# A two-layer encoder trunk: the second FFN product in one chunk of eleven tile pairs, with right factors kept in DRAM

## The chip, the cores and the metric

The kernel runs on one core of a Trainium2 chip. The metric is device microseconds (us) of one execution. TensorE (PE) multiplies, PEld is its weight load, VectorE is DVE, ScalarE is ACT, GpSimd is POOL and SyncE is SP; SyncE's queue issues nearly all DMAs.

## The reference, cut to what matters

The trunk has two layers on a sequence of 1024 tokens of width 1024, in float32. A layer is a normalisation, a projection into three kinds of mixers, an output projection, and then the part in which the change lies (`D_FF` is 2816, that is 22 tiles of 128):

```
h = rmsnorm(x, ffn_norm[i])
gu = h @ w_up[i]
x = x + (jax.nn.silu(gu[..., :D_FF]) * gu[..., D_FF:]) @ w_down[i]
x = x + (p[i] @ ple_proj[i]) * jax.nn.sigmoid(x @ ple_gate[i])
```

## The kernel before, in words

Everything is held transposed: features on the 128 partitions, tokens on the free axis in two halves of 512. A float32 operand is split into two parts of the type fp32r (`split`, L131): ScalarE casts the high part (L133), VectorE or, where `eng` says so, GpSimd subtracts it from the source to give the low part (L134). A product of two split operands takes three matmuls of 128 x 128 by 128 x 512, high by high, high by low and low by high (L1409 to L1411, and L219 to L221 in `product`).

The first FFN product (`feed` L1417, `up` L1285) makes one tile f of the 22 at a time. It uses a seven-product scheme on 2 x 2 blocks: seven sums (`part`, L1262) of 12 matmuls in place of eight. `factors` makes the seven left factors of the next tile meanwhile: its sums on GpSimd (L191 to L200), its splits on ScalarE and VectorE, in slots `wf` of the pool `big` (16 slots of 128 x 1024). For the tiles one to three the first two sums are made early (`heads`), so that five remain. The gated product of a tile, two halves of 128 x 512, is stored to the DRAM tensor `gd` (L1306).

The second FFN product (`lower`, L1309) is also made by seven products, on pairs of tiles, in two chunks of ten tiles (`NDOWN`). A chunk has the products 1, 2, 7, 5, 6, 3 and 4, each over five pairs, and a step (chunk, product, pair) is 12 matmuls into four PSUM banks. `fetch` loads the blocks of w_down (`a11` to `a22`, the left side) and of the gated product (`b11` to `b22`, the right side). `factors` inside `lower` forms a step's sums of blocks (L1336), `ready` splits the left one with GpSimd and the right one with VectorE, and the loop runs `ready` three steps (`DEEP`) ahead of the matmuls. After a product, `out` adds the four banks to blocks of x or to `sums` (L1382), and after product six of the second chunk adds `sums` to three blocks each (L1393). The two tiles left over are multiplied plainly, 96 matmuls (L219 to L221 with `g` and `wh`, added at L1479); at the end of this each block of x is split into `xp`, the right side of the gate's product that follows (`pe` and `pd` with `xp`).

Each engine runs its own queue in a fixed order. Tiles of a pool share its slots; a new tile waits until the last reader of the slot's former one is done. The framework orders the queues when the kernel is built, from the order of the code, its own estimates of durations and the free slots, so loads and splits can stand far ahead of where the code has them: loads of x that `lower` issues (L1376) go out while the first product still runs. SyncE's DMA instructions wait on SyncE's queue for their sources or slots, and those behind them wait too.

Of the kernel before, what the change touches and what calls it, by code (L numbers as in the profile page):

```python
# [21 lines left out]
P = 128  # L22
# [17 lines left out]
NDOWN = 10  # L40
# [42 lines left out]
class Trunk:  # L83
# [236 lines left out]
    def scratch(self):  # L320
        self.xd = self.dram.tile([KT, P, S], F32, name="xd")
        self.ya = self.dram.tile([3, P, S], F32, name="ya")
        self.yd = self.dram.tile([S, HC * HD], F32, name="yd")
        self.sgd = self.dram.tile([3, P, S], F32, name="sgd")
        self.gd = self.dram.tile([NFF, P, S], F32, name="gd")
        self.md = self.dram.tile([64, S], F32, name="md")
        self.ad = self.dram.tile([64, NCH], F32, name="ad")
# [704 lines left out]
    def plan_all(self):  # L1032
        t = self.t
        for li in range(DEPTH):
# [8 lines left out]
            for i in range(2):  # L1043
                self.plan((4, 256), t["w_last"][li, 4 * i : 4 * i + 4].rearrange("f p c -> p f c"))
# [240 lines left out]
    def up(self, rt, f, ops, gu):  # L1285
# [18 lines left out]
        for hf, (g, t) in enumerate(((g0, u), (g1, v))):  # L1304
            add(g, g, t, OP.mult)
            nc.sync.dma_start(self.gd[f][:, hf * 512 : hf * 512 + 512], g)  # L1306
        yield

    def lower(self, li, x, gp):  # L1309
# [4 lines left out]
        K2 = NDOWN // 2  # L1314
        where = {"11": (0, h0), "12": (K2, h0), "21": (0, h1), "22": (K2, h1)}
        raw = {}

        def fetch(c, *names):
            for k in range(K2):
                for n in names:  # L1320
                    if n in ("a12", "a22"):
                        if k % 2 == 0:
                            pair = self.slot("wr")
                        w = pair[:, k % 2 * 512 : k % 2 * 512 + 512]
                    else:
                        w = self.rhs.tile([P, 512], F32, tag="hl", name=self.nm("wr"))
                    if n[0] == "a":
                        k0, cs = where[n[1:]]
                        nc.sync.dma_start(w, t["w_down"][li, c * NDOWN + k0 + k, :, cs])
                    else:  # L1330
                        k0, cs = {"11": (0, h0), "12": (0, h1), "21": (K2, h0), "22": (K2, h1)}[n[1:]]
                        nc.sync.dma_start(w, self.gd[c * NDOWN + k0 + k][:, cs])
                    raw[c, n, k] = w

        def sub(out, a, b, eng=nc.vector, op=OP.subtract):
            eng.tensor_tensor(out, a, b, op)  # L1336
            return out

        def factors(c, m, k):

            g = lambda n: raw[c, n, k]
            p = lambda n: raw.pop((c, n, k))
            if m == 1:
                return g("a11"), g("b11")
            if m == 2:
                return g("a12"), g("b21")
            if m == 7:
                return sub(self.half("s"), g("a11"), g("a21")), sub(self.half("s"), g("b22"), g("b12"))
            if m == 5:
                return (sub(g("a21"), g("a21"), g("a22"), op=OP.add), sub(g("b12"), g("b12"), p("b11")))  # L1350
            if m == 6:
                return sub(g("a11"), p("a21"), g("a11")), sub(g("b12"), g("b22"), g("b12"))
# [4 lines left out]
        def ready(c, m, k):  # L1357
            l, r = factors(c, m, k)
            out = []
            for src, eng in ((l, nc.gpsimd), (r, nc.vector)):  # L1360
                pair = tuple(gp.tile([P, 512], F32R, tag="hl", name=self.nm("f")) for _ in range(2))
                self.split(pair, src, eng=eng)
                out.append(pair)
            if m == 3:
                raw.pop((c, "a12", k)), raw.pop((c, "b22", k))
            if m == 4:
                raw.pop((c, "a22", k)), raw.pop((c, "b21", k)), raw.pop((c, "b12", k))
            if k == K2 - 1 and c == 0:
                fetch(1, *{5: ("b11",), 6: ("a11",), 3: ("b21", "a12"), 4: ("a21", "b22", "b12", "a22")}.get(m, ()))
            return out  # L1370

        fetch(0, "a11", "b11")
        fetch(0, "a12", "b21")
        x += [self.slot("x") for _ in range(KT)]
        for o in range(KT):
            nc.sync.dma_start(x[o], self.xd[o])  # L1376
        us = [self.slot("u") for _ in range(2)]
        fetch(0, "a21", "b22", "b12", "a22")
        sums = [us[o // 2][:, o % 2 * 512 : o % 2 * 512 + 512] for o in range(4)]
# [4 lines left out]
        def out(c, m, o, ps):  # L1384
            c11, c12, c21, c22 = x[o][:, h0], x[o][:, h1], x[o + 4][:, h0], x[o + 4][:, h1]
            if m == 1 and c == 0:
# [9 lines left out]
        ahead = []  # L1396
        for i in range(len(steps) + DEEP):
            if i < len(steps):
                ahead.append(ready(*steps[i]))
            if i < DEEP:  # L1400
                continue
            c, m, k = steps[i - DEEP]
            if k == 0:
                odd = ((i - DEEP) // K2) % 2
                banks = [self.bank("pd", "d" if odd and o > 1 else "a") for o in range(4)]
            (lh, ll), (rh, rl) = ahead.pop(0)
            for o, ps in enumerate(banks):
# [3 lines left out]
                nc.tensor.matmul(ps, ll[:, cs], rh, start=False, stop=k == K2 - 1)  # L1411
            del lh, ll, rh, rl
            if k == K2 - 1:
                for o, ps in enumerate(banks):
                    out(c, m, o, ps)

    def feed(self, li, x, acc, rt, gp, fill):  # L1417
# [19 lines left out]
        x.clear()  # L1437
        for f in range(NFF):
# [13 lines left out]
        self.lower(li, x, gp)  # L1452
        self.limit = 1 << 30
        gs = self.pairs(2, "g", gp)
        for f, g in enumerate(gs):
            for hf in hs:
                gr = self.half("gr")
                nc.sync.dma_start(gr, self.gd[2 * NDOWN + f][:, hf * 512 : hf * 512 + 512])
                self.split(g[hf], gr)

        pp = self.pairs(PLE // P, "p", gp)
        for k in range(PLE // P):
            for hf in hs:
                pr = self.half("pr")
                nc.sync.dma_start(pr, t["p"][li, k, :, hf * 512 : hf * 512 + 512])
                self.split(pp[k][hf], pr)
        pw = self.pairs(2, "pw", gp)
        for i in range(4):
            pr = self.half("pr")
            nc.sync.dma_start(pr.rearrange("p (f c) -> p f c", f=2), t["ple_proj"][li, 2 * i : 2 * i + 2].rearrange("f p c -> p f c"))  # L1470
            self.split(pw[i // 2][i % 2], pr)
        xp = [[None, None] for _ in range(KT)]
        hl = [self.take(), self.take()]
# [193 lines left out]
```

## Time and profile before

| | |
|---|---|
| median of 3 runs (lowest to highest) | 2799.74 us (2798.83 to 2800.63) |
| the profiled execution, its span | 2797.81 us, 2796.0 us |
| PE busy, share of the span | 2670.7 us, 96% |
| DVE, ACT, POOL busy | 1920.4, 1129.1, 966.8 us |
| mean granted TensorE clock | 0.978 |
| DMA traffic | 258.57 MB, mean 92 GB/s |

Busy is the union of an engine's instructions. Matmuls overlap in their pipeline, so their starts tell the pace better than their durations. In the profile L1306 is line 1306 of the kernel. A wait is idle time of an engine in front of an instruction, put down to the instruction that ended it.

### The profile page before, as it was taken

What the parts mean: (1) busy time and instruction counts of PE and PEld (TensorE: products, weight loads), DVE (VectorE), ACT (ScalarE), POOL (GpSimd) and SP (SyncE); (2) the same over time, 40 slices, a digit from 0 to 9 for tenths busy, and PEclk for the clock granted to TensorE, in tenths of its full rate; (3) what the DMA queues carried; (4) which work ended last, traced back from release to release, by engine and by line L of the source; (5) the groups of instructions that cost most, each with busy time, mean ns of one, the idle gap of its engine ahead of it and who ended that gap; (6) DMA issues with size and microseconds to landing.
All of it is one profiled execution on the core that took longest, in us unless ns stands there. A gap on an engine that the chain in (4) does not pass through costs nothing.

```text
span 2796.0 us, 37474 instructions
## 1 busy us (share of the span) xinstructions
PE 2670.7 (96%) x13930; PEld 2124.0 (76%) x13930; DVE 1920.4 (69%) x3019; ACT 1129.1 (40%) x2301; POOL 966.8 (35%) x724
## 2 busy tenths in 40 slices
PE   8999998998999999999999999989899999989997
PEld 6777776676888887788777778857678888877887
DVE  8654866579665558997655448564986565599957
ACT  5443253544333324344445433543443333333444
POOL 3112433136332325660121123431553333276302
PEclk9999999999999999999999999999899999999999
DMA  4010145132222235312321012542232222632124
GB/s 146 28 65 31 42 110 174 56 129 72 95 77 82 91 109 189 116 61 68 114 82 54 32 38 71 116 148 97 79 113 76 83 91 72 207 133 86 46 83 136
DMA packets 134618, 258.57 MB, mean 92 GB/s; under 512 B 14649, under 2 KB 55649, under 8 KB 134436
## 3 DMA queue, kind: packets, MB, share of 16 engines
q1 hardware_dynamic: 130740, 244.51, 26.7%
q0 software_dynamic: 3696, 11.66, 1.2%
q8 instruction: 110, 1.80, 0.3%
q14 instruction: 72, 0.59, 0.1%
HBM read 206.19 MB, written 49.93 MB: 92 GB/s over the span
## 4 chain that ended last, share of the span: by engine, by line
PE 77%; DVE 12%; issue 4%; POOL 2%; ACT 2%; DMA 2%; SPq 0%; DVEq 0%; POOLq 0%; ACTq 0%
PE pd L219 10%; PE pd L220 9%; PE pd L221 9%; PE pd L1270 9%; PE pd L1269 9%; PE pd L1271 9%; PE pd L1410 3%; PE pd L1411 3%; PE pd L1409 3%; PE po L584 1%; PE ppt L563 1%; DVE f L134 1%; DVE x L1234 1%; DVE x L1382 1%; DVE wr L1336 1%
## 5 line engine op out<-in xcount | busy, mean ns | idle before, releaser
L1270 PE MATMUL pd<-r,wf 128*128 128x512 f32 x1232 | 494.0, 401 | 16.4 <-POOL r L1229 9.3
L1269 PE MATMUL pd<-r,wf 128*128 128x512 f32 x1232 | 490.1, 398 | 11.3 <-ACT r L1228 11.3
L1271 PE MATMUL pd<-r,wf 128*128 128x512 f32 x1232 | 488.9, 397 | 0.0
L219 PE MATMUL pd<-h,wh 128*128 128x512 f32 x832 | 339.3, 408 | 12.7 <-ACT h L133 6.8
L220 PE MATMUL pd<-h,wh 128*128 128x512 f32 x832 | 329.4, 396 | 2.8 <-DVE h L134 1.7
L221 PE MATMUL pd<-h,wl 128*128 128x512 f32 x832 | 328.0, 394 | 1.0 <-DVE wl L134 1.0
L1288 DVE TENSOR_TENSOR g<-g,pd 128x512 f32<-128x512 f32 x264 | 176.8, 684 | 219.0 <-PE pd L1271 218.9
L1270 PEld LDWEIGHTS pd<-r,wf 128*128 128x128 f32 x1232 | 234.7, 191 | 81.7 <-POOL r L1229 19.2
L1269 PEld LDWEIGHTS pd<-r,wf 128*128 128x128 f32 x1232 | 235.1, 191 | 67.0 <-ACT r L1228 13.0
L1271 PEld LDWEIGHTS pd<-r,wf 128*128 128x128 f32 x1232 | 235.3, 191 | 52.3
L134 POOL TENSOR_TENSOR f<-wr,f 128x512 fp32r<-128x512 f32 x120 | 181.2, 1523 | 154.7 <-ACT f L133 127.9
L1410 PE MATMUL pd<-f,f 128*128 128x512 f32 x560 | 221.3, 395 | 12.9 <-DVE f L134 12.9
L1409 PE MATMUL pd<-f,f 128*128 128x512 f32 x560 | 220.3, 393 | 5.4 <-DVE x L1382 5.4
L1411 PE MATMUL pd<-f,f 128*128 128x512 f32 x560 | 220.8, 394 | 4.2 <-POOL f L134 4.1
L133 ACT CAST f<-wr 128x512 fp32r<-128x512 f32 x240 | 137.9, 619 | 192.6 <-PE pd L1410 90.7
L133 ACT CAST wf<-s 128x512 fp32r<-128x512 f32 x176 | 105.0, 619 | 272.4 <-POOL s L200 121.1
L134 DVE TENSOR_TENSOR wf<-s,wf 128x512 fp32r<-128x512 f32 x176 | 176.2, 1002 | 42.8 <-ACT wf L133 41.6
L134 POOL TENSOR_TENSOR wl<-wr,wh 128x1024 fp32r<-128x1024 f32 (+1 forms) x44 | 109.3, 2483 | 249.9 <-ACT wh L133 139.5
L219 PEld LDWEIGHTS pd<-h,wh 128*128 128x128 f32 x832 | 158.0, 190 | 48.1 <-ACT h L133 6.8
L220 PEld LDWEIGHTS pd<-h,wh 128*128 128x128 f32 x832 | 158.0, 190 | 35.2 <-DVE h L134 2.6
L221 PEld LDWEIGHTS pd<-h,wl 128*128 128x128 f32 x832 | 157.7, 189 | 35.5 <-DVE wl L134 1.9
L197 POOL TENSOR_TENSOR s<-wr,s 128x512 f32<-128x512 f32 x44 | 59.1, 1344 | 307.1 <-DVE wf L134 307.1
(315 smaller groups left out, 5484.2 us busy)
## 6 DMA issues: line engine op xcount, KB each, us to landing
wr<-w_up SPq DMA_DIRECT2D x88, 512.0 KB, 3.7
wr<-w_in SPq DMA_DIRECT2D x52, 512.0 KB, 3.6
gd<-g SPq DMA_DIRECT2D x88, 256.0 KB, 2.0
wr<-w_down SPq DMA_DIRECT2D x80, 256.0 KB, 4.2
wr<-gd SPq DMA_DIRECT2D x80, 256.0 KB, 5.3
wr<-ple_gate SPq DMA_DIRECT2D x40, 512.0 KB, 3.5
ee<-md SPq DMA_DIRECT2D x32, 384.0 KB, 7.5
x<-xd SPq DMA_DIRECT2D x24, 512.0 KB, 4.3
```

The source lines that it names most:

```text
L133: self.pin(nc.scalar.copy(hi[:, cs], src))
L134: self.pin((eng or nc.vector).tensor_tensor(lo[:, cs], src, hi.bitcast(F32)[:, cs], OP.subtract))
L219: nc.tensor.matmul(ps, hi[:, ks], rh, start=k == 0, stop=False)
L220: nc.tensor.matmul(ps, hi[:, ks], rl, start=False, stop=False)
L221: nc.tensor.matmul(ps, lo[:, ks], rh, start=False, stop=k == n - 1)
L1269: nc.tensor.matmul(ps, hi[:, ks], rh, start=k == 0, stop=False)
L1270: nc.tensor.matmul(ps, hi[:, ks], rl, start=False, stop=False)
L1271: nc.tensor.matmul(ps, lo[:, ks], rh, start=False, stop=k == KT // 2 - 1)
L1288: add = lambda out, a, b, op=OP.add: nc.vector.tensor_tensor(out, a, b, op)
L1409: nc.tensor.matmul(ps, lh[:, cs], rh, start=k == 0, stop=False)
L1410: nc.tensor.matmul(ps, lh[:, cs], rl, start=False, stop=False)
L1411: nc.tensor.matmul(ps, ll[:, cs], rh, start=False, stop=k == K2 - 1)
```

## The change

The second product becomes one chunk of eleven pairs: tiles 2k and 2k + 1 form pair k, and the plain product of two tiles with its weights (`w_last`) is gone. The four sums of right blocks are no longer formed in `lower`. As soon as both tiles of a pair are gated, the generator `rights`, which runs in steps beside the next tile's sums, stores the raw blocks `b11`, `b21` and `b22` to the DRAM tensor `bd`, forms the four sums on VectorE, splits them on ScalarE and VectorE and stores them to the DRAM tensor `bs`. In `lower`, `right` loads a raw block into a half slot (products 1, 2 and 3, split there) or a made and split factor straight into `f` tiles (products 7, 5, 6 and 4), one step ahead of `ready`. The left splits and the left subtractions of product 3, on GpSimd before, are on VectorE. x is loaded in eight parts during the first two products. The embedding's operands, the first loads of the gate's weights and twelve of sixteen `xp` splits are made beside product four (`beside`), the last four `xp` splits after it.

```
+    def rights(self, i):
+        (b11, b12), (b21, b22) = self.gated
+        for n, b in enumerate((b11, b21, b22)):
+            nc.sync.dma_start(self.bd[i, n], b)
+        yield
+        for n, (out, a, b) in enumerate(((None, b22, b12), (b12, b12, b11), (b12, b22, b12), (b21, b21, b12))):
+            w = self.slot("wf", F32R)
+            hl = w[:, 0:512], w[:, 512:1024]
+            out = hl[1].bitcast(F32) if out is None else out
+            nc.vector.tensor_tensor(out, a, b, OP.subtract)
+            self.split(hl, out)
+            nc.sync.dma_start(self.bs[i, n], w.bitcast(F32))
+            yield
...
+        def left(m, k):
...
+            if m == 7:
+                return sub(self.half("s"), g("a11"), g("a21"))
+            if m == 5:
+                return sub(g("a21"), g("a21"), g("a22"), OP.add)
+            if m == 6:
+                return sub(g("a11"), p("a21"), g("a11"))
             if m == 3:
-                return sub(g("a12"), g("a12"), p("a11"), nc.gpsimd), g("b22")
-            return g("a22"), sub(g("b21"), g("b21"), g("b12"), nc.gpsimd)
+                w = p("a12")
+                return sub(w, w, p("a11"))
+            return p("a22")
+        def right(m, k):
+            if m in (1, 2, 3):
+                r = self.half("b")
+                nc.sync.dma_start(r, self.bd[k, m - 1])
+                return r
+            hl = tuple(gp.tile([P, 512], F32R, tag="hl", name=self.nm("f")) for _ in range(2))
+            for w, cs in zip(hl, (h0, h1)):
+                nc.sync.dma_start(w.bitcast(F32), self.bs[k, {7: 0, 5: 1, 6: 2, 4: 3}[m]][:, cs])
+            return hl
...
-            for src, eng in ((l, nc.gpsimd), (r, nc.vector)):
-                pair = tuple(gp.tile([P, 512], F32R, tag="hl", name=self.nm("f")) for _ in range(2))
-                self.split(pair, src, eng=eng)
+            for src in (left(m, k), r):
+                if not isinstance(src, tuple):
+                    pair = tuple(gp.tile([P, 512], F32R, tag="hl", name=self.nm("f")) for _ in range(2))
+                    self.split(pair, src)
...
-            for dst in {1: (sums[o], c11)[c == 0 :], 2: (c11,), 7: (c21, c22), 5: (c12, c22), 6: (sums[o],), 3: (c12,),
-                        4: (c21,)}[m]:
+            for dst in {1: (c11,), 2: (c11,), 7: (c21, c22), 5: (c12, c22), 3: (c12,), 4: (c21,)}.get(m, ()):
                 add(dst, ps)
-            if m == 6 and c == 1:
+            if m == 6:
+                add(sums[o], ps)
                 for dst in (c21, c12, c22):
-                    nc.vector.tensor_tensor(dst, dst, sums[o], OP.add)
-        steps = [(c, m, k) for c in range(2) for m in (1, 2, 7, 5, 6, 3, 4) for k in range(K2)]
+                    add(dst, sums[o])
+        steps = [(m, k) for m in (1, 2, 7, 5, 6, 3, 4) for k in range(NPAIR)]
...
+            if i + 1 < len(steps):
+                rs.append(right(*steps[i + 1]))
             if i < len(steps):
-                ahead.append(ready(*steps[i]))
+                ahead.append(ready(*steps[i], rs.pop(0)))
+                m, k = steps[i]
+                if m in (1, 2, 7):
+                    fetch({1: "a12", 2: "a21", 7: "a22"}[m], k)
+                if m in (1, 2) and k < 4:
+                    stream(4 * (m - 1) + k)
+            elif i == len(steps):
+                next(beside)
...
+                if m == 3:
+                    next(beside)
...
             for _ in self.up(rt, f, ops[-5:], gu):
                 next(fill, None)
+                next(rights, None)
             drain(fill)
+            drain(rights)
+            if f % 2:
+                rights = self.rights(f // 2)
+        drain(rights)
...
-                drain(self.product(hl[o // 4], gs, hf, ps, (o % 4) * 256))
-                nc.vector.tensor_tensor(x[o][:, cs], x[o][:, cs], ps, OP.add)
...
+        self.lower(li, x, gp, beside())
+        for o in range(4, KT):
+            operand(o, 0)
```

## Rows read from the trace of the kernel before

**Rows 1.** The page's busy times: engine, busy us, share of the span, instructions.
```profile
PE 2670.7 (96%) x13930; PEld 2124.0 (76%) x13930; DVE 1920.4 (69%) x3019; ACT 1129.1 (40%) x2301; POOL 966.8 (35%) x724
```

**Rows 2.** VectorE's timeline, first product: start, us, instruction, [idle before].
```profile
873.39 1.79 DVE L134 TENSOR_TENSOR wf<-s,wf 128x512 fp32r<-128x512 f32 x1
...
876.12 0.69 DVE L1282 TENSOR_TENSOR g<-g,pd 128x512 f32<-128x512 f32 x1 [0.34 <-PE pd L1271]
...
895.45 0.69 DVE L1282 TENSOR_TENSOR g<-g,pd 128x512 f32<-128x512 f32 x1 [0.34 <-PE pd L1271]
```

**Rows 3.** TensorE's timeline: first matmuls of second and gate's products.
```profile
1063.79 0.39 PE L1409 MATMUL pd<-f,f 128*128 128x512 f32 x1
...
1293.92 0.39 PE L219 MATMUL pe<-p,pw 128*128 128x512 f32 x1
...
2432.34 0.39 PE L1409 MATMUL pd<-f,f 128*128 128x512 f32 x1
...
2661.26 0.39 PE L219 MATMUL pe<-p,pw 128*128 128x512 f32 x1
```

**Rows 4.** Groups, whole span: xcount, busy us, mean ns, idle us before.
```profile
L1409 PE MATMUL pd<-f,f 128*128 128x512 f32 x560 | 220.3, 393 | 5.4 <-DVE x L1382 5.4
...
L219 PE MATMUL pd<-g,wh 128*128 128x512 f32 x64 | 25.3, 395 | 0.0
```

**Rows 5.** TensorE's waits, second product, layers 0 and 1: us, times, longest.
```profile
PE pd L1410 <- DVE f L134: 6.2, 4, 3.8
PE pd L1409 <- DVE x L1382: 3.3, 1, 3.3
PE pd L1411 <- POOL f L134: 2.7, 3, 1.3
...
PE pd L1410 <- DVE f L134: 6.7, 5, 2.6
PE pd L1409 <- DVE x L1382: 2.1, 1, 2.1
PE pd L1411 <- POOL f L134: 1.4, 2, 1.0
```

**Rows 6.** Second product: length, busy (count) of PE, PEld, DVE, ACT, POOL, clock, DMA.
```profile
1060.00:1272.00 212.00, 199.75 (x860) 162.10 (x860) 202.37 (x231) 87.98 (x154) 134.58 (x88) 0.98 0.33 110
```

**Rows 7.** Groups in the second product of layer 0, 1064 to 1271 us.
```profile
L134 POOL TENSOR_TENSOR f<-wr,f 128x512 fp32r<-128x512 f32 x56 | 85.0, 1531 | 41.2 <-ACT f L133 28.4 <-DVE f L134 7.2 <-DVE wr L1336 1.7
L134 DVE TENSOR_TENSOR f<-wr,f 128x512 fp32r<-128x512 f32 x56 | 63.4, 1148 | 1.4 <-ACT f L133 1.4
...
L1336 DVE TENSOR_TENSOR wr<-wr,wr 128x512 f32<-128x512 f32 x40 | 44.2, 1128 | 0.4
```

**Rows 8.** VectorE's timeline, second product, layer 0.
```profile
1244.09 2.98 DVE L1393 TENSOR_TENSOR x<-x,u 128x512 f32<-128x512 f32 x3
...
1265.92 2.48 DVE L134 TENSOR_TENSOR g<-gr,g 128x512 fp32r<-128x512 f32 x4
```

**Rows 9.** Stretches, columns as in rows 6: two of the first product, two later.
```profile
673.00:718.00 45.00, 45.00 (x195) 36.61 (x196) 39.92 (x53) 16.96 (x31) 22.65 (x17) 1.00 0.33 113
850.00:869.33 19.33, 19.33 (x86) 15.77 (x85) 11.53 (x17) 6.01 (x10) 6.27 (x4) 1.00 0.22 81
...
1233.50:1272.00 38.50, 38.50 (x172) 31.86 (x171) 35.93 (x48) 18.85 (x32) 13.47 (x10) 1.00 0.27 83
...
1030.00:1090.00 60.00, 60.00 (x264) 49.21 (x263) 39.08 (x44) 20.52 (x36) 22.39 (x15) 1.00 0.79 270
```

**Rows 10.** SyncE's queue in the first product.
```profile
875.85 0.81 SPq L157 DMA_DIRECT2D wr<-w_up  x2
```

**Rows 11.** DMA issues, 672 to 1064 us: count, KB each, median us to landing.
```profile
wr<-w_up SPq DMA_DIRECT2D x36, 512.0 KB, 3.7
...
wr<-gd SPq DMA_DIRECT2D x11, 256.0 KB, 6.5
```

**Rows 12.** GpSimd's timeline in the first product.
```profile
892.28 1.68 POOL L191 TENSOR_TENSOR s<-wr 128x512 f32<-128x512 f32 x1 [1.46 <-DVE wf L134]
```

More of the change, by code (lines that the diff above doesn't have):

```diff
@@ L324, in scratch @@
         self.sgd = self.dram.tile([3, P, S], F32, name="sgd")
-        self.gd = self.dram.tile([NFF, P, S], F32, name="gd")
+        self.bd = self.dram.tile([NPAIR, 3, P, 512], F32, name="bd")
+        self.bs = self.dram.tile([NPAIR, 4, P, S], F32, name="bs")
         self.md = self.dram.tile([64, S], F32, name="md")
@@ L1312, in lower @@
+    def lower(self, li, x, gp, beside):
         nc, t = self.nc, self.t
         h0, h1 = slice(0, 512), slice(512, 1024)
-        K2 = NDOWN // 2
-        where = {"11": (0, h0), "12": (K2, h0), "21": (0, h1), "22": (K2, h1)}
         raw = {}
[L1318 to L1333, printed above, removed]
@@ L1335, in sub, with place, fetch @@
-        def sub(out, a, b, eng=nc.vector, op=OP.subtract):
-            eng.tensor_tensor(out, a, b, op)
-            return out
-        def factors(c, m, k):
-            g = lambda n: raw[c, n, k]
-            p = lambda n: raw.pop((c, n, k))
+        spare = []
+        def place():
+            if not spare:
+                pair = self.slot("wr")
+                spare.extend((pair[:, h1], pair[:, h0]))
+            return spare.pop()
+        def fetch(n, k):
+            w = place() if n == "a22" or (n, k) == ("a12", NPAIR - 1) else self.rhs.tile([P, 512], F32, tag="hl", name=self.nm("wr"))
+            nc.sync.dma_start(w, t["w_down"][li, 2 * k + int(n[2]) - 1, :, h0 if n[1] == "1" else h1])
+            raw[n, k] = w
@@ new lines, in ready @@
+        def ready(m, k, r):
+            out = []
+            for src in (left(m, k), r):
+                if not isinstance(src, tuple):
+                    pair = tuple(gp.tile([P, 512], F32R, tag="hl", name=self.nm("f")) for _ in range(2))
+                    self.split(pair, src)
+                    src = pair
+                out.append(src)
+            return out
+        for k in range(NPAIR):
+            fetch("a11", k)
+        us = [self.slot("u") for _ in range(2)]
+        sums = [us[o // 2][:, o % 2 * 512 : o % 2 * 512 + 512] for o in range(4)]
@@ L1482, in feed, with operand, beside @@
-        del gs, hl
+        xp = [[None, None] for _ in range(KT)]
+        def operand(o, hf):
+            xp[o][hf] = tuple(self.rhs.tile([P, 512], F32R, tag="hl", name=self.nm("xp")) for _ in range(2))
+            self.split(xp[o][hf], x[o][:, hf * 512 : hf * 512 + 512])
+        pp, pw = [], []
+        def beside():
+            prs = []
+            for k in range(PLE // P):
+                for hf in hs:
+                    prs.append(self.half("pr"))
+                    nc.sync.dma_start(prs[-1], t["p"][li, k, :, hf * 512 : hf * 512 + 512])
+            for o in range(4):
+                for hf in hs:
+                    operand(o, hf)
+            for o in range(4, KT):
+                operand(o, 1)
+            yield
+            self.limit = 1 << 30
+            self.load(self.njob)
+            pp.extend(self.pairs(PLE // P, "p", gp))
+            for k in range(PLE // P):
+                for hf in hs:
+                    self.split(pp[k][hf], prs.pop(0))
+            pw.extend(self.pairs(2, "pw", gp))
+            for i in range(4):
+                pr = self.half("pr")
+                nc.sync.dma_start(pr.rearrange("p (f c) -> p f c", f=2), t["ple_proj"][li, 2 * i : 2 * i + 2].rearrange("f p c -> p f c"))
+                self.split(pw[i // 2][i % 2], pr)
+            yield
@@ L1485, in feed @@
+        self.lower(li, x, gp, beside())
+        for o in range(4, KT):
+            operand(o, 0)
         hn = [[None, None] for _ in range(KT)]
```

86 lines of the change are left out of this document (24 added, 62 removed).

## The prediction

> **What bounds the kernel now.** I read the busy times first, then where the two FFN products begin and end, then TensorE's waits in them, then what the engine that it waits for is doing. TensorE is busy for 96% of the span [rows 1]. A sum of matmul durations would overstate its work, because matmuls overlap; what counts is start to start. In the first FFN product one tile's 84 matmuls recur every 895.45 - 876.12 = 19.33 us [rows 2], so one matmul costs 19.33 / 84 = 0.2301 us. In the second product that pace isn't held. With the plain product behind it, it runs in layer 0 from 1063.79 to 1293.92, 230.13 us, and in layer 1 from 2432.34 to 2661.26, 228.92 us [rows 3]. Each layer has 936 matmuls there: three lines of 560 and three of 64 for both layers [rows 4]. At 0.2301 us that is 215.4 us, so 14.7 us and 13.5 us, together 28.2 us, are lost. The waits name their cause: 12.2 us in layer 0 and 10.2 us in layer 1 end on a VectorE or GpSimd split or on a VectorE addition [rows 5]; the rest is matmuls at a reduced pace behind them (granted clock 0.98 over the stretch [rows 6]). The engine that is short is VectorE, busy for 202.4 of 212 us, beside a GpSimd busy for 134.6 us [rows 6].
>
> **The change, part by part.** *Fewer matmuls.* Eleven pairs in one chunk make 7 x 11 x 12 = 924 matmuls for 936. Two layers save 24 x 0.2301 = 5.5 us, all on the path.
>
> *VectorE and GpSimd in the second product.* GpSimd's 70 splits of some 1.53 us and its 20 subtractions go. VectorE's split averages 1.15 us there and its subtraction 1.13 us [rows 7]; where GpSimd rests, four splits take 2.48 us, 0.62 us each [rows 8]. The new stage issues on VectorE 77 left and 33 right splits, 44 left subtractions, 48 additions (twelve per output block where 22 were), 16 splits for the gate's product, 8 for the embedding, and 8 operations of the last pair's right factors: 234 x 0.62 = 145 us of 924 x 0.2301 = 212.6 us, 68% where it was 95%. A step of twelve matmuls (2.76 us) has at most three of them, 1.9 us, in product three; product seven's step had two subtractions and a split, 3.4 us, and additions besides. So the cause of [rows 5] goes. ScalarE has some 142 operations of about 0.62 us, 88 us, as now [rows 6].
>
> One rule of the Trainium skill bears on that price. The row first: the same split takes 0.62 us alone [rows 8] and 1.15 us on average beside GpSimd [rows 7]. "SBUF — State Buffer", section "Who interferes with whom", says that a VectorE instruction with two SBUF inputs and a GpSimd instruction that reads SBUF contend for a port pair held as an exclusive lock, and that the second to issue waits for the whole of the first. By that rule the 0.62 us holds in the second product, where GpSimd falls silent, but not in the first, where GpSimd still works; what would follow there is rival B.
>
> *Right factors in the first product.* Every pair of tiles adds four subtractions and four splits on VectorE. Alone they cost 8 x 0.62 = 5.0 us; each caught beside GpSimd, as a split of 1.79 us [rows 2], 14.3 us. VectorE is busy 11.53 of 19.33 us per tile [rows 9], so a pair has 15.6 us free: even the dear end fits. GpSimd works 6.27 of the 19.33 us, a third, so I take 5.0 us plus a third of the difference, 8 us, and at this place no time. What covers it: six PSUM banks take the sums, and weight splits stand ahead of their use. The exception is the start: from 673 to 718 us VectorE is busy 39.9 of 45 us [rows 9], and the first pair falls there. If its 5.0 to 14.3 us don't fit into those 5.1 us, TensorE waits up to 9 us per layer; I take 2, by the near end.
>
> *SyncE.* A pair now issues seven stores for four. The new wait is that of a store for its split; behind it on the queue stand the next loads of w_up. They go out at 875.85 [rows 10] and land in 3.7 us [rows 11]; GpSimd's sum is the first to read them, a tile's period later at 892.28 [rows 12]. That leaves 12.7 us against a chain of subtraction, cast and split of under 5 us. Cost nothing; without that cover a wait of a few us per pair.
>
> *Hand-over to the second product.* It is seamless now: the last matmul of the one is followed by the first of the other [rows 3]. The last pair's right factors stand ahead of it on VectorE with 5.0 to 14.3 us; three prepared steps give TensorE 8.3 us. Bounds 0 to 6 us a layer; I take 1.
>
> *Right factors read back.* In products seven, five, six and four they come ready made, two loads of 256 KB a step. The buffers hold the running step and three more, 8.3 us; a load of that size lands in 6.5 us where the queue is fullest, at the hand-over [rows 11]. The stage reads 33 x 0.262 + 44 x 0.524 + 44 x 0.262 + 8 x 0.524 = 47.4 MB (right factors raw and made, w_down, x), 223 GB/s over 212.6 us. The trace has 270 GB/s over 60 us around the hand-over, with TensorE busy throughout [rows 9]. Bounds 0 to 3 us a layer; I take 1.
>
> *Behind product six* sixteen additions stand in one block, some 10 us against 8.3 us prepared: up to 3 us. The second chunk has the same block now (part of it at 1244.09 [rows 8]), and TensorE is busy for all of the stretch around it, 38.50 us [rows 9], since VectorE can work more than three steps ahead. I take 1.
>
> *Into the gate's product.* The plain product of 96 matmuls covered the embedding's splits, the first gate weights and the xp splits. Their cover is now product four, whose step needs 0.62 of 2.76 us on VectorE: 12 of the 16 xp splits and 8 others, 12.4 us, fit into its 30 us. The last four blocks need an addition, a cast and a split behind the last matmul, under 3 us, and are read behind six and twelve other matmuls, 4.1 us. Bounds 0 to 3 us; I take 0.5.
>
> **Sum.** 5.5 + 28.2 = 33.7 us at most. Given back per layer: 2 + 1 + 1 + 1 + 0.5 = 5.5 us, 11 us for both; bounds 0 and 24 us a layer. The profiled execution took 2797.81 us, its span 2796.0 and 1.8 us around it: 2797.8 - 33.7 + 11 = 2775 us. The median of the runs shown is 1.9 us above that execution, so I predict 2777 us as a median, and 2766 us with nothing given back.
>
> **Rivals.** *A (0.70), the sum above,* with 2764 to 2789 us as its own range.
>
> *B (0.12), the first product pays.* VectorE's new operations are caught behind GpSimd's, and on its queue they hold up weight splits and sums. For it: splits of 1.79 us in the steady part [rows 2], and 5.1 us free at the start [rows 9]. Against it: 15.6 us free per later pair. If the first two pairs cost 14.3 us each against some 5 us free, a layer loses 18.6 us where I took 2: 2777 + 33 = 2810 us; with one pair caught, 9.3 us where I took 2, 2792 us. It is the rule of the Trainium skill on "SBUF — State Buffer" that speaks for this case.
>
> *C (0.10), the waits stay in part.* They may lie in the order of the queues and not in VectorE's load. For it: the longest in layer 0 but one ended on an addition [rows 5], and blocks of additions remain. Against it: 3.4 us of work in steps of 2.76 us explains them. With half of the 28.2 us left, and 8 us of the other give-backs: 2799.7 - 33.7 + 14 + 8 = 2788 us; with the matmuls' 5.5 us alone, 2794 us.
>
> *D (0.08), slower: the loads pace the second product.* Place: SyncE's queue there. Price at 180 GB/s, two thirds of the 270 GB/s [rows 9], a supposition: 47.4 MB take 263 us where I have 213, so 50 us a layer and 2777 + 100 = 2877 us. It decides below 47.4 MB / 229.5 us = 207 GB/s, where the stage lasts as long as now. For it: twice the 110 GB/s of now [rows 6]. Against it: those 270 GB/s.
>
> **How the numbers follow.** Within 0.2%, 5.6 us, counts as no change; that is about what a measurement of this kernel can tell. Faster: A, 0.06 of B and 0.06 of C: 0.82. Same: 0.04 of C and 0.04 of B, between its two prices: 0.08. Slower: D and 0.02 of B: 0.10. The range runs from 2764 us (nothing given back, and 2 us for the spread of the runs) to 2797 us, which leaves out D and the dear half of B.
>
> **What would show it.** Right: the second product's 924 matmuls in 213 to 217 us a layer; no GpSimd work there; VectorE's splits at 0.62 to 0.7 us, and VectorE busy for about 70% of that stretch; 19.33 us per tile in the first product from the sixth tile on. Wrong: TensorE waiting in the first product on a cast or split of wf; TensorE or VectorE waiting in the second on a load from the new DRAM tensors; a gap of over 3 us at either hand-over.

## The result, and the profile after

The changed kernel takes 2762.05 us as a median of 4 runs (2759.57 to 2764.66), the kernel before beside it 2799.70; the ratio is 0.9866 with an interval of 0.9848 to 0.9883. The prediction was 2777 us with a range of 2764 to 2797: the direction is right, the gain of 37.6 us is more than the 22.7 us forecast, and the time lies 2 us below the range. The profiled execution took 2764.66 us, its span 2762.9 us.

The page's busy times of the changed kernel, columns as in [rows 1]:

```profile
PE 2653.5 (96%) x13906; PEld 2118.3 (77%) x13906; DVE 1874.0 (68%) x3119; ACT 1129.6 (41%) x2317; POOL 690.2 (25%) x544
```

GpSimd loses 180 instructions, 90 a layer. TensorE's timeline of the changed kernel has the first matmul of the second product and the first of the gate's product in each layer, as in [rows 3], here with the matmul ahead of each:

```profile
1064.74 0.40 PE L1271 MATMUL pd<-r,wf 128*128 128x512 f32 x1
1064.98 0.39 PE L1436 MATMUL pd<-f,f 128*128 128x512 f32 x1
...
1275.28 0.39 PE L1438 MATMUL pd<-f,f 128*128 128x512 f32 x1
1275.51 0.39 PE L219 MATMUL pe<-p,pw 128*128 128x512 f32 x1
...
2416.40 0.40 PE L1271 MATMUL pd<-r,wf 128*128 128x512 f32 x1
2416.63 0.39 PE L1436 MATMUL pd<-f,f 128*128 128x512 f32 x1
...
2627.19 0.39 PE L1438 MATMUL pd<-f,f 128*128 128x512 f32 x1
2627.42 0.39 PE L219 MATMUL pe<-p,pw 128*128 128x512 f32 x1
```

The second product takes 1275.51 - 1064.98 = 210.53 us and 2627.42 - 2416.63 = 210.79 us. Before it took 230.13 and 228.92 us [rows 3]: 19.6 + 18.1 = 37.7 us less, all of the gain. Both hand-overs are one matmul wide (0.24 and 0.23 us). The stretch between the first matmuls of the first and the second product is unchanged in both traces: 453.15 and 453.46 us before, 453.46 and 453.44 us after.

TensorE's waits in the second product of layer 0 (us in total, times, longest) are one line, where [rows 5] had three with 12.2 us:

```profile
PE pd L1437 <- DVE f L134: 0.3, 1, 0.3
```

The stretch inside it, columns as in [rows 6] (length; busy and count of PE, PEld, DVE, ACT, POOL; clock; DMA share; GB/s):

```profile
1065.00:1275.00 210.00, 209.54 (x923) 172.90 (x922) 144.47 (x231) 81.08 (x138) 0.00 (x0) 1.00 0.68 234
```

VectorE is busy for 144.5 us with 231 operations (145 us with 234 was forecast), GpSimd is silent, the granted clock is 1.00 for 0.98, and the loads move 234 GB/s for 110. The groups of the same stretch (as in [rows 7]) have the price of VectorE's operations without GpSimd beside them:

```profile
L134 DVE TENSOR_TENSOR f<-wr,f 128x512 fp32r<-128x512 f32 x64 | 43.7, 688 | 44.6 <-ACT f L133 42.6 <-DMA f<-bs 2.0
...
L133 ACT CAST f<-b 128x512 fp32r<-128x512 f32 x31 | 19.2, 619 | 16.5 <-DMA b<-bd 12.4 <-PE pd L1437 3.7 <-DVE f L134 0.2
L1346 DVE TENSOR_TENSOR wr<-wr,wr 128x512 f32<-128x512 f32 x33 | 20.8, 686 | 1.3 <-DMA wr<-w_down 1.3
```

A split takes 0.69 us for 1.15 and a subtraction 0.69 for 1.13. (144.47 / 231 is 0.625 us each, the price forecast from [rows 8]: operations in a row overlap a little.) ScalarE waited 12.4 us for raw blocks and VectorE 2.0 us, once, for a made factor; the prediction named the second as a sign of being wrong. No wait of TensorE ends on a load, and all its waits are 0.3 us: both lie within the three steps made ahead.

### The profile page after: what moved, and what is told of

Same layout as the page of the kernel before. It is cut to its first block, busy times and chain, and to the rows that moved or that the text cites. A ratio compares the mean times of both kernels' runs of the same rounds, so it can differ in the third digit from the quotient of the medians.

```text
span 2762.9 us, 37720 instructions
## 1 busy us (share of the span) xinstructions
PE 2653.5 (96%) x13906; PEld 2118.3 (77%) x13906; DVE 1874.0 (68%) x3119; ACT 1129.6 (41%) x2317; POOL 690.2 (25%) x544
## 4 chain that ended last, share of the span: by engine, by line
PE 82%; DVE 8%; issue 3%; DMA 2%; POOL 2%; ACT 2%; SPq 0%; DVEq 0%; POOLq 0%; ACTq 0%
PE pd L1270 9%; PE pd L1271 9%; PE pd L1269 9%; PE pd L219 9%; PE pd L220 9%; PE pd L221 9%; PE pd L1438 5%; PE pd L1437 5%; PE pd L1436 5%; PE po L586 1%; PE ppt L565 1%; DVE x L1234 1%; PE psc L709 1%; PE po L754 1%; PE psc L533 1%
## 5 line engine op out<-in xcount | busy, mean ns | idle before, releaser
L1270 PEld LDWEIGHTS pd<-r,wf 128*128 128x128 f32 x1232 | 233.8, 190 | 85.5 <-POOL r L1229 19.9
L1269 PEld LDWEIGHTS pd<-r,wf 128*128 128x128 f32 x1232 | 233.6, 190 | 66.0 <-ACT r L1228 12.6
L1437 PE MATMUL pd<-f,f 128*128 128x512 f32 x616 | 239.9, 389 | 1.1 <-DVE f L134 1.1
L1438 PE MATMUL pd<-f,f 128*128 128x512 f32 x616 | 239.7, 389 | 0.0
L1436 PE MATMUL pd<-f,f 128*128 128x512 f32 x616 | 236.3, 389 | 0.1
L134 DVE TENSOR_TENSOR wf<-s,wf 128x512 fp32r<-128x512 f32 x176 | 161.9, 921 | 64.1 <-ACT wf L133 63.0
L347 POOL TENSOR_TENSOR acc<-acc,sq 128x512 f32<-128x512 f32 (+1 forms) x22 | 29.6, 1344 | 654.5 <-ACT sq L346 654.2
L134 DVE TENSOR_TENSOR f<-wr,f 128x512 fp32r<-128x512 f32 x132 | 90.1, 688 | 90.4 <-ACT f L133 86.3
L133 ACT CAST wh<-wr 128x1024 fp32r<-128x1024 f32 (+1 forms) x112 | 113.7, 1016 | 70.8 <-PE pd L220 49.4
```

The source lines that it names most:

```text
L133: self.pin(nc.scalar.copy(hi[:, cs], src))
L134: self.pin((eng or nc.vector).tensor_tensor(lo[:, cs], src, hi.bitcast(F32)[:, cs], OP.subtract))
L1269: nc.tensor.matmul(ps, hi[:, ks], rh, start=k == 0, stop=False)
L1270: nc.tensor.matmul(ps, hi[:, ks], rl, start=False, stop=False)
L1436: nc.tensor.matmul(ps, lh[:, cs], rh, start=k == 0, stop=False)
L1437: nc.tensor.matmul(ps, lh[:, cs], rl, start=False, stop=False)
```

## The experiments

In the table, "second product" is start to start, as above, for layers 0 and 1; "lost" is that less the floor of the matmuls in it at the pace that the trace shows (section on the pace below); in e3 26 and in e5 2 matmuls of the gate's product a layer already stand in this stretch, and the floor counts them. "ratio" is to the kernel before, run on the same chip, which took 2799.6 to 2799.9 us there, and 2802.2 to 2802.3 us beside e8 and e10 to e13 below. All but e2 are the changed kernel with one edit; e2 is the kernel before with one edit.

| run | median us | ratio (interval) | second product, us | lost, us | VectorE there |
|---|---|---|---|---|---|
| before | 2799.70 | 1 | 230.1, 228.9 | 17.3, 16.1 | 260 op., 221 us |
| after | 2762.05 | 0.9866 (0.9848 to 0.9883) | 210.5, 210.8 | 1.1, 1.3 | 231, 145 us |
| e1 | 2766.58 | 0.9882 (0.9867 to 0.9897) | 212.5, 212.4 | 3.0, 2.9 | 156, 142 us |
| e2 | 2769.45 | 0.9890 (0.9873 to 0.9906) | 214.3, 214.3 | 1.5, 1.5 | 343, 209 us |
| e3 | 2781.87 | 0.9934 (0.9919 to 0.9949) | 224.9, 226.2 | 10, 11 | 339, 208 us |
| e4 | 2765.64 | 0.9878 (0.9863 to 0.9892) | 215.5, 212.3 | 6, 3 | 271, 168 us |
| e5 | 2796.46 | 0.9990 (0.9980 to 0.9999) | 228.4, 228.6 | 18, 19 | 377, 228 us |
| e9 | 2788.32 | 0.9958 (0.9944 to 0.9971) | 224.5, 225.5 | 15, 16 | 231, 190 us |
| e7 | 2774.93 | 0.9909 (0.9894 to 0.9924) | 217.2, 217.8 | 8, 8 | 231, 145 us |

**What ended the waits: VectorE's load, or GpSimd beside it?** The prediction named a short VectorE [rows 6]. The change takes away both, so the first runs take them apart.

e1_left_gpsimd gives the left splits back to GpSimd:

```
-            for src in (left(m, k), r):
+            for src, eng in ((left(m, k), nc.gpsimd), (r, nc.vector)):
...
-                    self.split(pair, src)
+                    self.split(pair, src, eng=eng)
```

> The changed kernel with its 77 left splits per layer on GpSimd again. Load theory: TensorE waited because VectorE had more work per step of twelve matmuls (2.72 us at 0.2267 us each) than fits. Then this costs little: VectorE has 157 operations per layer left in the second product, at most 1.15 us each beside GpSimd, 181 us of 209.5; no step exceeds 2.3 us. Second product 210 to 214 us a layer (210.5 in the changed kernel), total 2758 to 2772 us, ratio to before 0.985 to 0.990. Silence theory: it was GpSimd's working beside VectorE that made TensorE wait. Then 8 us or more a layer come back, total over 2778 us, ratio over 0.992.

Measured 2766.58 us, 3 us lost a layer. The groups of its second product, layer 0:

```profile
L134 POOL TENSOR_TENSOR f<-wr,f 128x512 fp32r<-128x512 f32 x64 | 93.6, 1469 | 73.6 <-ACT f L133 55.1 <-issue 8.3 <-DVE f L134 2.4
L134 DVE TENSOR_TENSOR f<-b,f 128x512 fp32r<-128x512 f32 x32 | 36.9, 1166 | 31.0 <-ACT f L133 29.7 <-POOL f L134 1.2
```

VectorE's split is back at 1.17 us, yet little is lost: with 156 operations VectorE has a third of the stage free. Contention alone doesn't make the waits.

e2_before_no_gpsimd is the kernel before with all of GpSimd's work in the second product on VectorE, so VectorE has more operations than before:

```
-                return sub(g("a12"), g("a12"), p("a11"), nc.gpsimd), g("b22")
-            return g("a22"), sub(g("b21"), g("b21"), g("b12"), nc.gpsimd)
+                return sub(g("a12"), g("a12"), p("a11")), g("b22")
+            return g("a22"), sub(g("b21"), g("b21"), g("b12"))
...
-            for src, eng in ((l, nc.gpsimd), (r, nc.vector)):
+            for src, eng in ((l, nc.vector), (r, nc.vector)):
```

> The kernel before with all splits and subtractions of the second product on VectorE, so that GpSimd rests there as in the changed kernel. Load theory: a step of products 7, 5 and 6 has two subtractions and two splits, 2.5 us, and its share of the additions, 1.0 us, 3.5 us against 2.72 us; VectorE's 308 operations of 0.62 us are 191 us for 190.4 us of matmuls. The waits stay: second product 202 to 215 us a layer (207.7 and 206.5 before), total 2785 to 2815 us, ratio 0.995 to 1.005. Silence theory: the waits go, second product 191 to 195 us a layer, total 2766 to 2777 us, ratio under 0.992.

The load theory missed. The stretch, columns as above:

```profile
1066.00:1276.00 210.00, 208.90 (x919) 172.03 (x919) 205.10 (x337) 91.33 (x159) 0.00 (x0) 1.00 0.32 103
```

VectorE is busy for 205 of 210 us, a larger share than before the change, with 343 operations a layer for 260, and TensorE loses 1.5 us a layer in place of 17. These three words in the old kernel bring 2799.7 - 2769.5 = 30 us of the 38; what is left, 7.4 us, is about what the change saves in matmuls (6.7 us, below).

e9_noise adds one GpSimd addition per step that nothing reads; VectorE's instructions stay the same 231:

```
+            (lh, _), _ = out
+            nc.gpsimd.tensor_tensor(self.half("s"), lh.bitcast(F32), lh.bitcast(F32), OP.add)
```

> The changed kernel with one GpSimd addition of 128x512 per step of the second product whose result nobody reads. VectorE's instructions are the same 231 per layer. If GpSimd makes VectorE's instructions longer (0.91 us on average beside GpSimd's left splits, 0.61 us alone), they take 200 to 240 us of 209.5: waits of 4 to 20 us a layer, total 2770 to 2800 us, ratio 0.990 to 1.000. If GpSimd's own splits were merely late (1.5 us each), noise costs nothing: 2757 to 2768 us, ratio under 0.989.

```profile
1066.00:1276.00 210.00, 199.85 (x862) 162.99 (x861) 177.29 (x218) 72.96 (x127) 108.45 (x71) 0.98 0.63 221
```

With GpSimd busy for 108 us of this stretch the same operations take 190 us a layer in place of 145, and 15 us a layer are lost again, at a VectorE that is busy for only 84% of the stretch. So its busy share doesn't tell: before 95% and 17 us lost, e2 98% and 1.5 us, e9 84% and 15 us. How much of the 15 us is the stretching alone is not shown: the added instruction also holds half slots and `f` tiles, and ScalarE's casts waited 12.6 us for it.

Which operations are stretched can be read from the groups: first one of the kernel before (1064 to 1271 us, as in [rows 7]), then two of e9 (1066 to 1270 us).

```profile
L1382 DVE TENSOR_TENSOR x<-x,pd 128x512 f32<-128x512 f32 x60 | 37.2, 673 | 0.0
```

```profile
L134 DVE TENSOR_TENSOR f<-wr,f 128x512 fp32r<-128x512 f32 x60 | 53.9, 909 | 19.7 <-ACT f L133 15.3 <-issue 4.3
...
L1402 DVE TENSOR_TENSOR x<-x,pd 128x512 f32<-128x512 f32 x28 | 17.5, 677 | 2.2 <-PE pd L1440 2.2
```

The additions from `pd`, with one input in PSUM, keep their 0.67 us beside GpSimd; the splits and subtractions, with both inputs in SBUF, go to 1.15 us before [rows 7] and 0.91 in e9. One by one, in the second product of layer 0 of the kernel before, those with both inputs in SBUF took 1.38 us on average where a GpSimd instruction overlapped them (85) and 0.68 where none did (63); those with an input in PSUM took 0.67 us either way (58 and 15). The Trainium skill's "SBUF — State Buffer", section "Who interferes with whom", has a VectorE instruction with two SBUF inputs and a GpSimd instruction that reads SBUF hold one port pair, each for its whole length; these numbers agree.

**How much VectorE can take when GpSimd rests.** e5_extra2 adds two subtractions per step to VectorE (they change the low part of a split, so that e5 no longer computes the trunk and only its time is of use):

```
+            (lh, ll), _ = out
+            for _ in range(2):
+                nc.vector.tensor_tensor(ll, ll.bitcast(F32), lh.bitcast(F32), OP.subtract)
```

> The changed kernel with two more VectorE operations per step of the second product (the left factor's low part is made three times). GpSimd stays silent there. Load theory, revised: what counts is VectorE's time product by product at the price it has, against 30.0 us of matmuls, less the lead that some five prepared steps give, 13.6 us. Sums at 0.61 us: 29, 29, 32, 32, 37, 36 and 35 us; 20 us too many, of which 10 to 13.6 us are lead: 6 to 10 us of waits a layer and some 2 us of slow matmuls behind them; total 2774 to 2790 us, ratio 0.991 to 0.997. Silence theory (GpSimd at work or not decides): 2757 to 2768 us, ratio under 0.989.

```profile
1066.00:1276.00 210.00, 199.62 (x854) 160.40 (x852) 209.90 (x350) 72.20 (x127) 0.00 (x0) 0.98 0.64 227
```

I undersized it: 377 operations keep VectorE busy for 228 us, and the stage takes 228.4. Steps made ahead cover a step that is late, not a sum that is above TensorE's 209.5 us.

e3_sums_in_place and e4_sums_unsplit undo the right factors: e3 stores only the four raw blocks and makes sums and splits in the second product, e4 stores the sums unsplit and splits them there.

```
+        for n, b in enumerate((b11, b21, b22, b12)):
...
+            if m in (5, 6, 4):
+                sub(rs[0], rs[0], rs[1])
+            if m in (6, 4):
+                sub(rs[0], rs[2], rs[0])
```

```
-            self.split(hl, out)
-            nc.sync.dma_start(self.bs[i, n], w.bitcast(F32))
+            nc.sync.dma_start(self.bs[i, n], out)
```

> The changed kernel, but the first product only stores the four raw blocks of a pair, and the right sums are formed and split on VectorE in the second product, as before the change; one chunk and a silent GpSimd stay. Load theory: 347 operations of 0.62 us are 215 us for 209.5 us of matmuls; steps of products 6 and 4 have five operations, 3.1 us against 2.72 us. Waits of 8 to 18 us a layer: second product 218 to 228 us, total 2775 to 2800 us, ratio 0.991 to 1.000. Silence theory, and the theory that one chunk instead of two does it: second product 210 to 213 us, total 2757 to 2767 us, ratio 0.985 to 0.988.

> The changed kernel with the right sums stored unsplit: half the bytes to and from the new DRAM tensor (23 MB less per layer), and 44 casts and 44 splits per layer move from the first product into the second. Load theory: 274 operations of 0.62 us, 170 us of 209.5, and no step over three operations, 1.9 us: no new wait, second product 210 to 213 us, total 2757 to 2767 us, ratio 0.985 to 0.988. If the split form is what matters, waits of 5 us or more a layer come back, total over 2772 us; if the traffic costs time now, the total falls below 2757 us.

e3 loses 10 to 11 us a layer with 208 us of VectorE work, e2 loses 1.5 us with 209: near the limit the load alone doesn't tell, and the order of the work is the likely reason. e3's work is uneven (product four has up to three subtractions a step and two splits); its one long wait stands behind product six, in product three:

```profile
PE pd L1437 <- DVE f L134: 4.7, 2, 4.2
```

e4, with 168 us, is 3.6 us above the change in its median, and the runs of the two overlap (2762.77 to 2768.80 beside 2759.57 to 2764.66). So making the sums early is worth some 20 us in this chunk, and splitting them early a few at most.

**The loads.** e7_twice loads each made factor twice:

```
+                nc.sync.dma_start(self.half("b"), self.bs[k, {7: 0, 5: 1, 6: 2, 4: 3}[m]][:, cs])
```

> The changed kernel with each made right factor loaded twice, the second time into a spare half slot that nobody reads: 70.5 MB instead of 47.4 MB per layer in the second product, 336 GB/s over 209.5 us. If the loads are the next bound (rival D), the stage lengthens to 70.5 MB at some 330 GB/s or less, 214 to 235 us a layer, total 2768 to 2815 us. If they are hidden with room to spare: 210 to 213 us, total 2757 to 2768 us, ratio under 0.989.

```profile
1066.00:1276.00 210.00, 206.16 (x894) 168.15 (x893) 139.76 (x224) 77.96 (x136) 0.00 (x0) 0.99 0.95 340
```

At 340 GB/s, a DMA share of 0.95, the stage lasts 217 us for 210.5; the change needs 234 GB/s. The added loads cost time only there (they also take half slots and places on SyncE's queue, which this run doesn't separate from their bytes). Rival D had the mechanism, and a bound (270 GB/s, from a stretch with a share of 0.79 [rows 9]) that was no limit.

**The pace of a matmul.** The changed second product is at 210.53 us for 924 matmuls below the 212.6 us that the prediction called its floor. TensorE's timeline of the kernel before has the reason, 2 us behind the place of [rows 3]; 28 starts are left out:

```profile
2434.17 0.39 PE L1411 MATMUL pd<-f,f 128*128 128x512 f32 x1
2434.40 0.39 PE L1409 MATMUL pd<-f,f 128*128 128x512 f32 x1
...
2440.97 0.39 PE L1411 MATMUL pd<-f,f 128*128 128x512 f32 x1
```

Thirty matmuls start in 2440.97 - 2434.17 = 6.80 us, 0.2267 us each. The 0.2301 us that I took from the first product is a mean of two paces, 226.7 and 233.3 ns. Of a tile's 84 matmuls there the 36 that stream t2, t3 or t4 from the pool of the `f` tiles run at 233.3; the rest, with weights and streamed tile both in lower pools, run at 226.7, but for the first five or so behind a slow part, which are up to 236 ns apart. In the second product both operands lie in that pool, and the pace is 226.7; in the plain product before, with weights in `big`, it was 233.3.

e6_swap puts t1 and b22 into that pool and t2 and t3 out of it:

```
-            put("t2", t2, k, gp)
+            put("t2", t2, k)
...
-            put("t1", x[k][:, h0], k)
+            put("t1", x[k][:, h0], k, gp)
```

> The changed kernel with the right factors t1 and b22 of the first product in the pool of 24 tiles and t2 and t3 in the pool of 32, the other way round than before. In the first product 36 of a tile's 84 matmuls (parts t2, t3, t4) start 0.233 us apart and the others 0.227 us. If it is the place of the streamed tile in SBUF that makes the difference, the parts t1, b22 and t4 are now the slow ones, still 36 of 84, and a tile still takes 19.33 us; if it is the part, t2, t3 and t4 stay slow. Either way the total stays within 6 us of the changed kernel, 2757 to 2768 us.

Measured 2764.09 us: the slow matmuls are now those of t1, b22 and t4. The pace goes with where the tile lies, not with its making. e8_side moves the pool of small tiles to the other end and the pool of `factors`' sums (`fs`) behind the `f` pool, so that the `f` pool begins at byte 150208 of a partition in place of 177824 (the places follow from the sizes of the pools ahead):

```
-        self.sm = ent(tc.tile_pool(name="sm", bufs=2))
+        self.sm = ent(tc.tile_pool(name="sm", bufs=2, side="right"))
...
-        with tc.tile_pool(name=f"fs{li}", bufs=2) as self.fs, tc.tile_pool(name=f"ffn{li}", bufs=24) as gp:
+        with tc.tile_pool(name=f"ffn{li}", bufs=24) as gp, tc.tile_pool(name=f"fs{li}", bufs=2) as self.fs:
```

> Place theory (the pace of a matmul, 226.7 or 233.3 ns, goes by where its streamed tile and its weights lie): of the 84 matmuls of one tile of the first product 36 stream t2, t3 or t4 out of the pool that begins at byte 177824 of a partition, at 233.3 ns. Here that pool begins at byte 150208, the pool of small tiles moves to the far end. If the border lies at or above 177824, all 36 run at 226.7: 36 x 6.6 ns x 44 tiles = 10.5 us less, first product 453.5 to about 448.5 us a layer, 2752 us. If the border lies at or below 150208: no change, 2762 to 2766. If it lies between: part of it, some tiles of t2, t3 and t4 fast and others slow, in order of their addresses, and the border is read from that: 2753 to 2762. Rival (the pace goes by the pool or by how many buffers it has, not by address): no change, 36 slow matmuls a tile as before.

2748.70 us, 0.9813 (0.9799 to 0.9828); first product 448.3 and 447.1 us, and from 700 to 1060 us no slow start is left, also from tiles beyond byte 177824. That is no border. The two begins differ in something else: 177824 leaves 32 when divided by 64, 150208 and the weights' pool leave 0. e12_pad and e13_side_pad cross place and remainder with a tile of 32 bytes ahead of the pool, e12 in the changed kernel, e13 in e8:

```
+        ... tc.tile_pool(name=f"pad{li}", bufs=1) as pad, tc.tile_pool(name=f"ffn{li}", bufs=24) as gp ...
+            nc.vector.memset(pad.tile([P, 8], F32, tag="pad", name=self.nm("pad")), 0.0)
```

> A tile of 32 bytes is put ahead of the pool of the streamed tiles t2, t3 and t4, which so begins at byte 177856 of a partition in place of 177824; the second product's pairs lie in it too. Alignment theory (a matmul takes 226.7 ns where its weights and its streamed tile lie at the same remainder by 64 bytes and 233.3 ns where they don't: 177824 leaves 32, the weights 0): all 36 slow matmuls of a tile become fast, first product 453.5 to about 448 us, second product unchanged at 210.6, 2748 to 2754 us as with the pool at byte 150208. Border theory (tiles beyond some byte are slow): no change, 2762 to 2766 us, since the pool lies where it lay.

> The pool of t2, t3 and t4 at the low place, with the same 32 bytes ahead of it: it begins at byte 150240 in place of 150208. Alignment theory: the 36 matmuls of a tile are slow again, first product 447.7 back to about 453 us, second product unchanged, 2758 to 2766 us. Border theory: all fast as with 150208, 2747 to 2752 us.

| `f` pool begins at byte | remainder by 64 | median us | first product, us | starts 230 to 240 ns apart, 700 to 1060 us |
|---|---|---|---|---|
| 177824 (after) | 32 | 2762.05 | 453.5, 453.4 | 823 of 1563 |
| 177856 (e12) | 0 | 2749.05 | 447.4, 448.0 | 0 of 1588 |
| 150208 (e8) | 0 | 2748.70 | 448.3, 447.1 | 0 of 1587 |
| 150240 (e13) | 32 | 2763.65 | 454.6, 454.6 | 826 of 1560 |

The twelve matmuls that stream t4 in the twelfth tile, in e12's timeline and in e13's:

```profile
866.20 0.39 PE L1270 MATMUL pd<-r,wf 128*128 128x512 f32 x1
866.42 0.39 PE L1271 MATMUL pd<-r,wf 128*128 128x512 f32 x1
...
868.69 0.39 PE L1272 MATMUL pd<-r,wf 128*128 128x512 f32 x1
```

```profile
870.38 0.39 PE L1270 MATMUL pd<-r,wf 128*128 128x512 f32 x1
870.61 0.40 PE L1271 MATMUL pd<-r,wf 128*128 128x512 f32 x1
...
872.95 0.40 PE L1272 MATMUL pd<-r,wf 128*128 128x512 f32 x1
```

From the first start to the twelfth it is 868.69 - 866.20 = 2.49 us in the one and 872.95 - 870.38 = 2.57 us in the other, 226 and 234 ns a matmul. The remainder decides, the place doesn't. The second product, whose two operands share their remainder in all four, takes 210.4 to 211.6 us in each. Whether the step is 64 bytes is not shown: where the pace is 226.7 ns, weights and streamed tile lie a multiple of 512 bytes apart, and where it is 233.3, 32 bytes off such a multiple, so 128, 256 or 512 would fit as well.

**The lesson carried to the first product's start.** There TensorE still waits 17 us a layer, and GpSimd works beside VectorE. e10_quiet_start gives all of GpSimd's work in making the right factors of the first product to VectorE; e11_both is e8 and e10 at once:

```
-                put("b11" if k < K2 else "b21", x[k][:, h0], k, eng=nc.gpsimd)
+                put("b11" if k < K2 else "b21", x[k][:, h0], k)
...
-            (nc.gpsimd if k % 2 else nc.vector).tensor_tensor(u[:, h0], u[:, h1], u[:, h0], OP.subtract)
+            nc.vector.tensor_tensor(u[:, h0], u[:, h1], u[:, h0], OP.subtract)
...
```

> All of GpSimd's work in making the first product's right factors (20 subtractions a layer) goes to VectorE; the rest as in the changed kernel. Contention theory (GpSimd's instructions delay VectorE's beside them): the waits of TensorE at this start, 17 us a layer, six of them 6.6 us on GpSimd's own instruction, fall although VectorE has 20 more instructions: at 0.7 us each these are 14 us spread over some 25 us of stage, and its present ones go from above 1 us to 0.7; waits 8 to 13 us a layer, in all 8 to 16 us less: 2746 to 2756. Load theory (VectorE paces the start): 20 x 0.7 to 1.1 us more on the engine that is late, waits 20 to 30 us a layer: 2768 to 2790.

> Both edits at once: if the two are independent, their differences from the changed kernel (2762 to 2766 us) add up within 2 us. By place and contention theory at their best 2736 to 2750; by their rivals 2768 to 2790.

e10 takes 2741.79 us, 0.9786 (0.9772 to 0.9800), 20 us below the change where 8 to 16 were expected. The start of the first product in the changed kernel and in e10, columns as above:

```profile
610.00:680.00 70.00, 53.00 (x188) 38.32 (x187) 69.14 (x74) 30.21 (x52) 49.54 (x29) 0.88 0.13 45
```

```profile
610.00:680.00 70.00, 58.79 (x231) 42.72 (x230) 69.75 (x102) 33.92 (x59) 19.26 (x13) 0.95 0.19 64
```

VectorE is busy for all of both, but gets 102 operations done for 74, and TensorE 231 matmuls for 188 (2.2 us of the 70 are an earlier start of the product in e10). The first product falls from 453.5 to 443.5 us a layer, the waits at its start from 17 to 11.2 and 10.2 us. The other 3 to 4 us a layer were missing from my expectation: behind the long waits 26 matmuls a layer started some 427 ns apart (the 1.2 GHz level, granted clock 0.88 in the stretch); in e10 it is 7 and 11 (0.95 in layer 0).

e11 takes 2729.64 us (2729.02 to 2730.45), 0.9742 (0.9729 to 0.9755): the two edits add up (13.4 + 20.3 = 33.7 us by the medians, 32.4 measured; in the first products of both layers, where the edits act, 11.5 + 19.9 = 31.4 us and 31.6), and it beats both kernels, the one before by 72.6 us on the same chip.

## Why the prediction was wrong

Its direction, its place and its mechanism held: all of the gain lies in the second product, GpSimd is silent there, VectorE's operations fell to 0.69 us (0.62 in a row), its load to 145 us, and the waits of [rows 5] went from 12.2 to 0.3 us. Against the time measured it is 15 us off, in four terms:

- *The step "at 0.2301 us that is 215.4 us", which priced the floor of the second product from the pace of the first,* failed. At the paces of the stage itself before has 840 x 0.2267 + 96 x 0.2333 = 212.8 us, so 17.3 and 16.1 us were lost, not 14.7 and 13.5; and 924 matmuls cost 209.5 us, 3.4 us a layer less than that. The most that the change could bring was 33.4 + 6.7 = 40.1 us, not 33.7: 6.4 us. This term also set the range's lower end, 2764 us for nothing given back, which would have been 2757.6. The starts shown above stood in the trace of before; I read the pace where the tile's period was easy to read. e6, e8, e12 and e13 show what sets it.
- *The step "given back per layer: 2 + 1 + 1 + 1 + 0.5"* was mis-sized: 11 us taken, 2.7 us measured. The first product gave back 0.3 us (2 a layer taken), and hand-over, loads, product six and the way into the gate's product 1.1 and 1.3 us a layer together (3.5 taken). What I had seen of each cover (six PSUM banks, 12.7 us on SyncE's queue, three steps) would have carried a price near nothing; the cautious values add up to 8.3 us too much.
- The rest of the kernel, which the change doesn't touch, took 4.3 us more in the profiled execution than before. From the first matmul of the gate's product in layer 0 to the first of the first product in layer 1 the profiled executions of kernels with the same code there (before, after, e1, e2, e4 to e13) take 684 to 688 us; 2.7 of the 4.3 us lie there, within that spread.
- The median lies 2.6 us below the profiled execution where I put it 1.9 above: 4.5 us the other way. That these two nearly cancel is luck.

6.4 + 8.3 - 4.3 + 4.5 = 14.9 us, the difference between 2777 and 2762.

The reading of the cause was half right. "The engine that is short is VectorE" [rows 6] named the engine but not why. The 3.4 us of work in a step of 2.76 us that it gave were three operations at the price beside GpSimd; at 0.62 us they are 1.9 us and fit. e2 gives VectorE more operations, and 1.1 us of waits are left; e1 leaves GpSimd at work, and with VectorE at two thirds only 3 us a layer are lost; e9 adds only GpSimd's work, and 15 us are lost again. The waits came from the two engines together: operations stretched to 1.1 us and more, on an engine without the room for it. Of the rivals, B came to nothing. VectorE's new groups in the changed kernel's first product, 680 to 1060 us, ten pairs:

```profile
L134 DVE TENSOR_TENSOR wf<-g,wf 128x512 fp32r<-128x512 f32 x30 | 28.7, 955 | 6.5 <-ACT wf L133 6.3
L1321 DVE TENSOR_TENSOR g<-g,g 128x512 f32<-128x512 f32 x30 | 21.1, 702 | 0.3
L134 DVE TENSOR_TENSOR wf<-wf 128x512 fp32r<-128x512 f32 x10 | 16.7, 1674 | 0.0
...
L1321 DVE TENSOR_TENSOR wf<-g,g 128x512 f32<-128x512 f32 x10 | 6.9, 692 | 9.6 <-POOL s L200 9.5
```

They are 73.4 us, 7.3 a pair (8 forecast); one split in four is caught behind GpSimd at 1.67 us, as the rival has it, but in time that VectorE had free, and no wait of TensorE lies there. C and D did not happen; e3 leaves room for C's mechanism, and e7 shows a rate at which D's could begin.

## What to carry to other kernels

Price a stage by the pace of its own matmuls, start to start, in the trace. An engine's busy share does not tell whether it is short: look at the mean of one operation beside another engine's work and alone, and where the two differ by much, try giving the work to the one engine before restructuring (here three words brought 30 of 38 us). Covers that the trace shows to be wide enough are priced at nothing, with the fear in the range and not in the sum.

## What was not expected of the hardware

- A 128 x 128 by 128 x 512 fp32r matmul followed its predecessor after 226.7 ns where weights and streamed tile lay at the same remainder by 64 bytes (0 and 0, or 32 and 32), and after 233.3 ns where one lay at 0 and the other at 32. 32 bytes of padding were worth 13 us of 2762, 11.5 of them in the first product. Other remainders were not tried, and a step of 128, 256 or 512 bytes would fit these runs as well. The Trainium skill's "SBUF — State Buffer", section "Who interferes with whom", lists the reads of streamed tile and weights as independent ports; these runs show that the two are not without effect on each other.
- The same 231 VectorE operations took 145 us beside a silent GpSimd and 190 us beside one at work for half of the time; VectorE's split took 0.69 and up to 1.79 us [rows 2], while additions with an input in PSUM kept 0.67 us.
- The loads reached 340 GB/s over 210 us beside running matmuls.
